# Expert bias as one-pass matmuls over stacked high and low rows; the rows of an expert gated and split when they leave PSUM

## The chip, the cores and the metric

The kernel runs on one core of a Trainium2 chip. The metric is the device time of one execution in microseconds. The engines are named as in the profile: PE is TensorE, DVE is VectorE, ACT is ScalarE, POOL is GpSimd, SP is SyncE, which here mostly issues DMAs.

## The reference, cut to what matters

Two transformer blocks run one after the other on 256 tokens of width 1024. The part that the change touches is the mixture of experts at the end of the first block: every token goes to 4 of 32 experts, each with 1024 x 2048 input weights, a bias of 2048, a clamped SwiGLU, and 1024 x 1024 output weights.

```python
logits = (hf @ w_router + b_router)
top_val, top_idx = lax.top_k(logits, TOP_K)
gates = jax.nn.softmax(top_val, axis=-1)
...
gu = xb @ w1[e] + b1[e]
gate = jnp.minimum(gu[:, :D_FF], SWIGLU_LIMIT)
up = jnp.clip(gu[:, D_FF:], -SWIGLU_LIMIT, SWIGLU_LIMIT)
act = (up + 1.0) * gate * jax.nn.sigmoid(SWIGLU_ALPHA * gate)
return (act @ w2[e] + b2[e]) * g[:, None]
...
out = jnp.zeros((n_tok, d), h.dtype).at[row_tok].add(y.reshape(n_rows, d))
```

All weights are float32: 12 MB for each expert, 32 experts.

## The kernel before, in words

The kernel has three stages. `block_pre` (mixing, memory attention) runs up to about 230 us of the trace; the experts (`route`, `expert_first`, `block_moe`) up to about 1207 us; `post_head` and `block_post` (the second block) after that.

**An expert.** At most 64 tokens (CAP) of an expert are gathered by one-hot matmuls (`gather`, L714, four experts at a time) into columns of 64. `expert_in` first puts the bias into two PSUM banks: four matmuls (L741), each with 32 rows of a selection matrix `bs` (one column of an identity, spread over 64 tokens by a DVE copy, L736) against 32 rows of `b1` (L620 loads it as four blocks of 512 columns, one in each quarter of the partitions). Then 8 weight tiles of 1 MB, 4 matmuls each (L746), are added to the same banks. `gemm1` evicts them (L808 to L812), transposes (L815) and copies (L817) the activations. `gemm2` multiplies them with 4 tiles of output weights, 1 MB each (L829), into one PSUM bank Y with 64 tokens on partitions 0 to 63 for the first 512 output columns and the same tokens on 64 to 127 for the rest. A float32 matmul shows as two records in the trace, a float32r matmul as one; matmuls on 64 columns are issued in pairs that take the two halves of the array.

**Combining.** `rows_out` copies Y to `ysb` on ACT (L834). `combine_weights` transposes the one-hot rows weighted by the gates (`ohw`, L788 on DVE; L800 on PE; L802 on ACT) into `cw`. After every second expert `combine` multiplies `cw` with the `ysb` of both (L845: 8 float32 matmuls on 64 rows, x 2 records) and adds the result to `x` on DVE (L848). The last pair is combined in `post_head` (L1112, L1087).

**Order.** The program order on PE is: input tiles of expert e, output tiles of expert e-1, `combine` after every second one. A list scheduler orders what does not depend, and so slips the bias of the next expert and a gather between other matmuls. SP issues the weight loads in the same order into 12 buffers of 1 MB (3 + 9, `new_w`); a load waits until the matmuls on the tile 12 loads earlier are done. After expert 15 all 12 tiles of expert 16 are loaded ahead and a branch (L880, `If`) skips the path for experts with over 64 tokens; it isn't taken here. `LAST = 2` moves half of the output tiles of expert 30 ahead of expert 31.

## Time and profile before

| | us |
|---|---|
| median of 3 runs | 1553.48 |
| the runs | 1548.6, 1559.29, 1553.48 |
| the profiled execution, and its span | 1548.9, 1547.1 |
| PE busy in the span | 1465.9 (95%) |
| DVE, ACT, POOL busy | 540.0, 384.2, 53.4 |
| moved by DMA | 486.31 MB, mean 314 GB/s |

A share of busy time is an average over the stages. The profile cuts the span into 40 slices of 38.7 us with a digit for each engine, the granted clock of PE and the rate of the DMAs; the experts fill slices 7 to 30. A matmul's end is modelled, so that PE counts as busy for about as long as it has something in flight; whether it waits is seen in the chain of waits.

### The profile page before, as it was taken

How to read it: one execution, taken by the hardware profiler on the slowest of the kernel's cores; microseconds unless marked ns; L12 is line 12 of the kernel's file. 1: busy time of each engine (PE TensorE's matmuls, PEld its weight loads, DVE VectorE, ACT ScalarE, POOL GpSimd, SP SyncE). 2: the span in 40 equal slices, each digit the busy share in tenths (PEclk: the TensorE clock that was granted, in tenths of full speed). 3: DMA queues.
4: the chain of work that ended last, by engine and by line, in shares of the span. 5: the costliest groups of instructions: out<-in, count | busy, mean ns of one | idle time of the engine just before them, and what ended most of it. 6: DMA issues, size and time to landing. Idle time of an engine off the chain costs nothing.

```text
span 1547.1 us, 20381 instructions
## 1 busy us (share of the span) xinstructions
PE 1465.9 (95%) x8440; PEld 798.0 (52%) x8440; DVE 540.0 (35%) x993; ACT 384.2 (25%) x783; POOL 53.4 (3%) x56
## 2 busy tenths in 40 slices
PE   9999999999999999998999999999999975889998
PEld 7899983333333333333333333223323774778998
DVE  5557652111221111121111111211111656985675
ACT  5845441100010010010001000000000553445654
POOL 0010000000000000000000000000000102500000
PEclk9999999999999999999999999999999997999999
DMA  9694347999999999998999999999998453332453
GB/s 336 222 317 164 116 171 285 419 415 417 418 417 413 414 417 416 416 414 343 413 415 419 417 416 417 418 418 415 418 416 334 140 111 98 110 123 94 154 192 108
DMA packets 146498, 486.31 MB, mean 314 GB/s; under 512 B 8606, under 2 KB 77342, under 8 KB 113505
## 3 DMA queue, kind: packets, MB, share of 16 engines
q1 hardware_dynamic: 143968, 479.10, 79.2%
q0 software_dynamic: 1504, 4.12, 1.4%
q10 hardware_dynamic: 928, 1.74, 0.4%
q8 instruction: 68, 1.11, 0.3%
q14 instruction: 30, 0.24, 0.0%
HBM read 481.78 MB, written 3.15 MB: 313 GB/s over the span
## 4 chain that ended last, share of the span: by engine, by line
PE 37%; issue 7%; DVE 5%; DMA 2%; ACT 2%; POOL 0%; POOLq 0%; ACTq 0%; DVEq 0%
PE pP L746 14%; PE pY L829 8%; PE pA L319 4%; PE pP L741 2%; PE pA L845 2%; DMA w<-in_w_in_dram 2%; DVE t L1378 2%; PE pA L714 1%; DVE t L1379 1%; PE pA L815 1%; PE pY L1323 1%; DVE r L1372 1%; DMA w<-in_w_expert_in_dram 0%; PE pP L1691 0%; DVE x L848 0%
## 5 line engine op out<-in xcount | busy, mean ns | idle before, releaser
L746 PE MATMUL pP<-w,xg 128*64 128x512 f32 x2024 | 448.6, 596 | 3.9 <-PEq L880 3.9
L746 PEld LDWEIGHTS pP<-w,xg 128*64 128x64 f32 x2024 | 144.5, 137 | 299.8 <-issue 285.7
L829 PE MATMUL pY<-w,hgu 128*64 128x512 f32 x1024 | 273.1, 606 | 0.7 <-ACT hgu L817 0.7
L209 ACT CAST wh<-w 128x512 fp32r<-128x512 f32 (+1 forms) x256 | 155.1, 615 | 156.2 <-PE pA L319 97.8
L210 DVE TENSOR_TENSOR wl<-w,wh 128x512 fp32r<-128x512 f32 x232 | 157.1, 688 | 76.3 <-ACT wh L209 73.3
L808 DVE TENSOR_SCALAR wh<-pP 128x512 f32<-128x512 f32 x32 | 22.1, 692 | 454.3 <-PE pP L746 454.3
L809 ACT ACTIVATE wh<-wh 128x512 f32<-128x512 f32 x32 | 20.2, 630 | 523.8 <-DVE wh L808 479.8
L829 PEld LDWEIGHTS pY<-w,hgu 128*64 128x64 f32 x1024 | 70.8, 137 | 152.9 <-issue 139.6
L319 PE MATMUL pA<-wh,xh 128*128 128x256 f32 x496 | 142.6, 287 | 4.1 <-DVE bk L1349 4.0
L319 PE MATMUL pA<-wh,xl 128*128 128x256 f32 x496 | 141.7, 286 | 0.0
L319 PE MATMUL pA<-wl,xh 128*128 128x256 f32 x496 | 140.7, 284 | 0.0
L319 PE MATMUL pA<-xh,wh 128*128 128x256 f32 x368 | 108.5, 295 | 4.5 <-ACT wh L209 2.3
L319 PE MATMUL pA<-xh,wl 128*128 128x256 f32 x368 | 106.8, 291 | 2.3 <-DVE wl L210 2.3
L319 PE MATMUL pA<-xl,wh 128*128 128x256 f32 x368 | 105.4, 287 | 0.0
L319 PEld LDWEIGHTS pA<-wh,xh 128*128 128x128 f32 x496 | 95.0, 192 | 5.8 <-issue 3.1
L845 PE MATMUL pA<-ysb,cw 64*128 64x512 f32 x240 | 74.8, 640 | 21.5 <-DVE x L848 11.7
L319 PEld LDWEIGHTS pA<-wl,xh 128*128 128x128 f32 x496 | 94.8, 191 | 0.4 <-issue 0.2
L319 PEld LDWEIGHTS pA<-wh,xl 128*128 128x128 f32 x496 | 94.7, 191 | 0.3 <-issue 0.2
L848 DVE TENSOR_TENSOR x<-pA,x 128x512 f32<-128x512 f32 x60 | 38.8, 686 | 151.1 <-PE pA L845 151.1
L741 PE MATMUL pP<-b,bs 32*64 32x512 f32 x256 | 87.5, 613 | 0.0
L319 PEld LDWEIGHTS pA<-xh,wh 128*128 128x128 f32 x368 | 71.3, 194 | 7.7 <-ACT wh L209 3.5
L319 PEld LDWEIGHTS pA<-xh,wl 128*128 128x128 f32 x368 | 71.3, 194 | 3.6 <-DVE wl L210 3.1
(425 smaller groups left out, 1418.4 us busy)
## 6 DMA issues: line engine op xcount, KB each, us to landing
w<-in_w_expert_in_dram SPq DMA_DIRECT2D x253, 1024.0 KB, 13.5
w<-in_w_expert_out_dram SPq DMA_DIRECT2D x128, 1024.0 KB, 13.1
w<-in_w_in_dram SPq DMA_DIRECT2D x31, 1024.0 KB, 5.4
w<-in_w_mem_kv_dram SPq DMA_DIRECT2D x8, 1024.0 KB, 12.0
w<-in_w_out_dram SPq DMA_DIRECT2D x8, 1024.0 KB, 6.3
w<-in_w_mem_q_dram SPq DMA_DIRECT2D x4, 1024.0 KB, 7.1
w<-in_w_mem_o_dram SPq DMA_DIRECT2D x4, 1024.0 KB, 5.2
w<-in_w_ple_gate_dram SPq DMA_DIRECT2D x4, 1024.0 KB, 4.8
```

Of the source, the lines that this page charges most:

```text
L209: nc.scalar.copy(wh, src)
L210: (nc.gpsimd if lo == "P" else nc.vector).tensor_tensor(wl, src, wh.bitcast(F32), op=ALU.subtract)
L319: nc.tensor.matmul(ps[:, j], lh, rh, start=n == 0, stop=n == tot - 1)
L714: nc.tensor.matmul(ps, xx[tt][:, k * P:(k + 1) * P], og[:, tt], start=n == 0, stop=n == 3)
L741: nc.tensor.matmul(out[i], bs[pr], K.b1[pr], start=True, stop=False, tile_position=(32 * i, 64 * (i % 2)))
L746: nc.tensor.matmul(out[i], xs, raw[:, i * 512:(i + 1) * 512], start=False, stop=k == KT - 1)
L808: nc.vector.tensor_scalar(g, Pb[0], 7.0, None, op0=ALU.min)
L809: nc.scalar.activation(sg, g, AF.Sigmoid, scale=1.702)
L829: nc.tensor.matmul(Y[64 * h:64 * h + 64], act[:, k % 4, k // 4], raw[:, j * 1024 + h * 512:j * 1024 + h * 512 + 512], start=k == 0, stop=k ...
L845: nc.tensor.matmul(pss[h], cws[i][pr, tt], ys[i][pr], start=i == 0, stop=i == 1)
L848: nc.vector.tensor_tensor(xs, pss[h], xs, op=ALU.add)
L1378: TT(pd[:, :, 0:n], BL[:, si:32, si][:, None, :].to_broadcast([P, 16, n]), U[:, si:32].rearrange("p s j -> p j s"), op=ALU.mult)
```

## The change

The bias comes in as two blocks of 1024 columns, each loaded twice (rows 0 to 63 and 64 to 127, 8 loads in place of 4, at the start of the kernel), into buffers that the one-hot rows use later. `bias_split` rounds them to float32r on ACT and leaves on the lower 64 partitions the rest (raw less rounded, on DVE). `bselc` has two columns for each expert, and the bias is two float32r matmuls on all 128 rows, which write 128 columns (both halves) at once.

`combine_weights` transposes the weighted one-hot rows once (64 columns, not 128), makes zeros and ones of them on DVE, copies these to the lower partitions on ACT, and sums the gate of each row on DVE. `rows_out` now scales Y by that gate as it leaves PSUM: for each half of the columns ACT writes the rounded rows (float32r) to 64 partitions and DVE writes the rest to the other 64 (`st`, 5 buffers). `combine` is 8 float32r matmuls on 128 rows. `post_head` does the same for the last pair.

```diff
@@ -52,7 +52,9 @@
     c["before"] = (i[:, None] < i[None, :]).astype(f)
     c["iota_e"] = np.tile(np.arange(NE, dtype=f), (P, 1))
     c["iota_s"] = np.tile(np.arange(CAP, dtype=f), (P, 1))
-    c["bselc"] = np.concatenate([np.eye(NE, dtype=f)] * 4)
+    eye = np.eye(NE, dtype=f)
+    none = np.zeros((NE, NE), f)
+    c["bselc"] = np.block([[eye, none], [none, eye], [eye, none], [none, eye]])
     band = np.zeros((P, 4, 3, P), f)
     for g, win in enumerate((2, 4, 8, 16)):
         full = np.zeros((T, T), f)
@@ -66,7 +68,7 @@
     return {"cpack": pack(c, CPACK), "bpack": pack(c, BPACK).astype(ml_dtypes.bfloat16), "band": band.reshape(P, -1)}
 
 
-WIDTH = {"iota_e": NE, "iota_s": CAP, "bselc": NE, "omask": 64}
+WIDTH = {"iota_e": NE, "iota_s": CAP, "bselc": 2 * NE, "omask": 64}
 
 
 class Pair:
@@ -434,6 +436,7 @@
     mem = K.new_w().rearrange("p (a d) -> p a d", a=2)
     nc.sync.dma_start(mem, A["mem"][0].rearrange("(a p) d -> p a d", p=P))
     moe_load(K, A)
+    bias_in(K, A)
     K.gemm(w_in, 1024, 4, xT, "N", ev_vu, pre=pre_w)
 
     es = []
@@ -576,6 +579,7 @@
     K.gemm(A["w_mem_q"][0], 0, 4, hT, "T", ev_Q, il=True)
 
     ple_load(K, A)
+    bias_split(K)
     ssx2 = K.t([P, 2, 4], F32, "ssx", 2)
     K.hTr = K.t([P, KT, T], F32, "qk", 1)
     lg = K.bank("P", (P, 2, NE))
@@ -611,13 +615,25 @@
 EB = 6
 LAST = 2
 FILL0 = 6
+NST = 5
 
 
 def bias_in(K, A):
     nc = K.nc
-    b1 = K.b1 = K.m([P, 512], F32, "b1", 1)
-    for i in range(4):
-        nc.scalar.dma_start(b1[32 * i:32 * i + 32], A["b_expert_in"][0][:, 512 * i:512 * i + 512])
+    b1 = K.b1 = K.m([P, 2, 512], F32R, "b1", 1)
+    K.b1raw = [K.m([P, 512], F32, "ohr", 2) for _ in range(2)]
+    for b in range(2):
+        for i in range(4):
+            o = 1024 * b + 512 * (i % 2)
+            nc.scalar.dma_start(K.b1raw[b][32 * i:32 * i + 32], A["b_expert_in"][0][:, o:o + 512])
+
+
+def bias_split(K):
+    nc = K.nc
+    lo = slice(64, P)
+    for b, raw in enumerate(K.b1raw):
+        nc.scalar.copy(K.b1[:, b], raw)
+        nc.vector.tensor_tensor(K.b1[lo, b], raw[lo], K.b1[lo, b].bitcast(F32), op=ALU.subtract)
 
 
 def route(K, x, lg, finish):
@@ -732,13 +748,12 @@
 
 def expert_in(K, A, e, spare={}):
     nc = K.nc
-    bs = K.m([P, CAP], F32, "bs", 2)
-    nc.vector.tensor_copy(bs, K.c["bselc"][:, e:e + 1].to_broadcast([P, CAP]))
+    bs = K.m([P, 2, CAP], F32R, "bs", 2)
+    nc.vector.tensor_copy(bs, K.c["bselc"].rearrange("p (j e) -> p j e", j=2)[:, :, e:e + 1].to_broadcast([P, 2, CAP]))
     Pb = [K.bank("P") for _ in range(2)]
     out = [Pb[i // 2][64 * (i % 2):64 * (i % 2) + 64] for i in range(4)]
-    for i in range(4):
-        pr = slice(32 * i, 32 * i + 32)
-        nc.tensor.matmul(out[i], bs[pr], K.b1[pr], start=True, stop=False, tile_position=(32 * i, 64 * (i % 2)))
+    for b in range(2):
+        nc.tensor.matmul(Pb[b], bs.rearrange("p j c -> p (j c)"), K.b1[:, b], start=True, stop=False)
     for k in range(KT):
         raw = spare[k] if k in spare else load_in(K, A, e, k)
         xs = K.XG[e // 4, k][:, e % 4]
@@ -779,13 +794,13 @@
 
     Ys = {}
     OHG = {}
+    cwg = {}
 
     def weigh(g):
-        ow = K.t([P, 2, 4, 2, CAP], F32, "ohw", 2)
-        for tt in range(2):
-            gb = G[:, tt, 4 * g:4 * g + 4, None, None].to_broadcast([P, 4, 2, CAP])
-            og = K.OG[g][:, tt].bitcast(F32)[:, :, None, :].to_broadcast([P, 4, 2, CAP])
-            nc.vector.tensor_tensor(ow[:, tt], og, gb, op=ALU.mult)
+        ow = K.t([P, 2, 4, CAP], F32, "ohw", 2)
+        for tt in range(2):
+            gb = G[:, tt, 4 * g:4 * g + 4, None].to_broadcast([P, 4, CAP])
+            nc.vector.tensor_tensor(ow[:, tt], K.OG[g][:, tt].bitcast(F32), gb, op=ALU.mult)
         OHG[g] = ow
 
     def make_group(g):
@@ -795,12 +810,16 @@
 
     def combine_weights(e):
         g, j = e // 4, e % 4
-        ps = K.bank("A", (P, 2, P))
-        for tt in range(2):
-            nc.tensor.transpose(ps[:, tt], OHG[g][:, tt, j].rearrange("p a b -> p (a b)"), c["ident"])
-        cw = K.t([P, 2, P], F32, "cw", 4)
-        nc.scalar.copy(cw, ps)
-        return cw
+        ps = K.bank("A", (CAP, 2, P))
+        for tt in range(2):
+            nc.tensor.transpose(ps[:, tt], OHG[g][:, tt, j], c["ident"])
+        cw = K.t([P, 2, P], F32R, "cw", 4)
+        gate = K.t([P, 1], F32, "gate", 4)
+        nc.vector.tensor_scalar(cw[0:64], ps, 0.0, None, op0=ALU.is_gt)
+        nc.scalar.copy(cw[64:P], cw[0:64].bitcast(F32))
+        nc.vector.reduce_sum(gate[0:64], ps, axis=AX.XY)
+        nc.scalar.copy(gate[64:P], gate[0:64])
+        return cw, gate
 
     def gemm1(e, spare={}):
         Pb = K.Pb if e == 0 else expert_in(K, A, e, spare)
@@ -829,23 +848,15 @@
                     nc.tensor.matmul(Y[64 * h:64 * h + 64], act[:, k % 4, k // 4], raw[:, j * 1024 + h * 512:j * 1024 + h * 512 + 512],
                                      start=k == 0, stop=k == KT - 1)
 
-    def rows_out(e):
-        y = K.t([P, 512], F32, "ysb", 3)
-        nc.scalar.copy(y, Ys.pop(e))
-        return y
-
     def combine(e):
-        cws = [combine_weights(e - 1), combine_weights(e)]
-        ys = [K.yprev, rows_out(e)]
-        for tt in range(2):
-            pss = [K.bank("A") for _ in range(2)]
-            for i in range(2):
-                for h in range(2):
-                    pr = slice(64 * h, 64 * h + 64)
-                    nc.tensor.matmul(pss[h], cws[i][pr, tt], ys[i][pr], start=i == 0, stop=i == 1)
+        pair = K.yprev, rows_out(K, Ys.pop(e), cwg.pop(e))
+        for tt in range(2):
             for h in range(2):
+                ps = K.bank("A")
+                for i, (cw, st) in enumerate(pair):
+                    nc.tensor.matmul(ps, cw[:, tt], st[h], start=i == 0, stop=i == 1)
                 xs = x[:, tt, h * 512:(h + 1) * 512]
-                nc.vector.tensor_tensor(xs, pss[h], xs, op=ALU.add)
+                nc.vector.tensor_tensor(xs, ps, xs, op=ALU.add)
 
     half = K.nexp // 2 - 1
     prev = None
@@ -863,14 +874,16 @@
         if e % 4 == 3 and e + 1 < K.nexp:
             make_group(e // 4 + 1)
         if prev is not None:
+            cwg[e - 1] = combine_weights(e - 1)
             gemm2(e - 1, prev, ahead2, range(LAST if last else 0, 4))
             ahead2 = {}
             if (e - 1) % 2 == 1:
                 combine(e - 1)
             else:
-                K.yprev = rows_out(e - 1)
+                K.yprev = rows_out(K, Ys.pop(e - 1), cwg.pop(e - 1))
         prev = act
         if e == half:
+            cwg[e] = combine_weights(e)
             gemm2(e, act)
             combine(e)
             prev = None
@@ -880,14 +893,26 @@
             with K.tc.If(cnt > CAP):
                 dense_rest(K, A, x, xh, xl, pos, G, iota_e, g_f)
     last = K.nexp - 1
-    cw = [combine_weights(last - 1), combine_weights(last)]
+    K.cwg = combine_weights(last)
     K.xT = [K.bank("P", (P, 2, T)) for _ in range(4)]
     for k in range(KT):
         for tt in range(2):
             nc.tensor.matmul(K.xT[k // 2][:, k % 2, tt * P:(tt + 1) * P], x[:, tt, k * P:(k + 1) * P], c["ident"],
                              start=k % 2 == 0 and tt == 0, stop=False)
     gemm2(last, prev)
-    K.cw, K.Y = cw, Ys[last]
+    K.Y = Ys[last]
+
+
+def rows_out(K, Y, cwg):
+    cw, gate = cwg
+    st = []
+    for h in range(2):
+        t = K.t([P, 512], F32R, "st", NST)
+        a, b = (slice(64 * i, 64 * i + 64) for i in (h, 1 - h))
+        K.nc.scalar.mul(t[a], Y[a], gate[a])
+        K.nc.vector.scalar_tensor_tensor(t[b], Y[a], gate[a], t[a].bitcast(F32), op0=ALU.mult, op1=ALU.subtract)
+        st.append(t)
+    return cw, st
 
 
 def dense_rest(K, A, x, xh, xl, pos, G, iota_e, g_f):
@@ -1057,7 +1082,6 @@
     c = K.c
     TS, mm = nc.vector.tensor_scalar, nc.tensor.matmul
     w_in = A["w_in_2"][0]
-    y = K.t([P, 512], F32, "ysb", 3)
     s = K.s = K.g([P, 2], F32, "s", 1)
     hs = K.hs = K.g([P, 2], F32, "hs", 1)
     u = K.u = Pair(K)
@@ -1082,9 +1106,8 @@
 
     def spread(tt, h):
         ps = K.bank("Y")
-        pr = slice(64 * h, 64 * h + 64)
-        for i, yy in enumerate((K.yprev, y)):
-            mm(ps, K.cw[i][pr, tt], yy[pr], start=i == 0, stop=i == 1)
+        for i, (cw, st) in enumerate(pair):
+            mm(ps, cw[:, tt], st[h], start=i == 0, stop=i == 1)
         queue.append((ps, x[:, tt, h * 512:(h + 1) * 512]))
 
     def add():
@@ -1103,14 +1126,11 @@
         nc.vector.tensor_tensor(x[:, tt], x[:, tt], gfB, op=ALU.mult)
 
     with K.tc.manual_schedule(engines={nc.scalar.engine, nc.vector.engine}):
-        nc.scalar.copy(y, K.Y)
-        for j in range(4):
-            for h in range(2):
-                k = 4 * h + j
-                pr = slice(64 * h, 64 * h + 64)
-                for i, yy in enumerate((K.yprev, y)):
-                    mm(K.xT[k // 2][:, k % 2], yy[pr, j * P:(j + 1) * P], K.cw[i][pr].rearrange("p a b -> p (a b)"),
-                       start=False, stop=k % 2 == 1 and i == 1)
+        pair = K.yprev, rows_out(K, K.Y, K.cwg)
+        for k in range(KT):
+            for i, (cw, st) in enumerate(pair):
+                mm(K.xT[k // 2][:, k % 2], st[k // 4][:, k % 4 * P:k % 4 * P + P], cw.rearrange("p a b -> p (a b)"),
+                   start=False, stop=k % 2 == 1 and i == 1)
         split(0)
         split(1)
         spread(0, 0)
@@ -1712,7 +1732,6 @@
         xp = K.extra(XW, XH)
         ph = K.phase("pre")
         x, lg, finish = block_pre(K, A)
-        bias_in(K, A)
         with route(K, x, lg, finish):
             expert_first(K, A)
         post_gains(K)
```

**PE, the bias of the next expert, after the input tiles of one expert and around the first output tile of the one before it** (`bs`, `b`: selection and bias; `hgu`: activations; `ohw`: weighted one-hot rows; `pP`, `pY`, `pA`: PSUM banks). Before:

```order
L746 MATMUL pP_3653<-w_3700,xg_3600 64x512 x2
L741 MATMUL pP_3874<-b_397_2522,bs_3872 64x512 x2
L741 MATMUL pP_3875<-b_397_2522,bs_3872 64x512
L829 MATMUL pY_3721<-w_3722,hgu_3565 64x512
L815 MATMUL pA_3714<-cpack_120,wh_3707 128x128 x4
L829 MATMUL pY_3721<-w_3722,hgu_3565 64x512 x3
L800 MATMUL pA_3746<-cpack_120,ohw_3101 128x128 x2
L800 MATMUL pA_3751<-cpack_120,ohw_3101 128x128 x2
L741 MATMUL pP_3875<-b_397_2522,bs_3872 64x512
```

In the changed kernel:

```order
L761 MATMUL pP_3942<-w_3987,xg_3642 64x512 x2
L756 MATMUL pP_4231<-b_77_484,bs_4229 128x512
L756 MATMUL pP_4232<-b_77_484,bs_4229 128x512
L848 MATMUL pY_4017<-w_4018,hgu_3897 64x512 x3
L834 MATMUL pA_4001<-cpack_120,wh_3994 128x128 x4
L815 MATMUL pA_4008<-cpack_120,ohw_3662 64x128 x2
L848 MATMUL pY_4017<-w_4018,hgu_3897 64x512
```

Four matmuls on 64 columns, one of them five places later than the others, become two on 128 columns in one place, and the transposes of `ohw` for this expert alone stand here.

**PE, combining, from the last output tile of an odd expert (`gemm2` ends just ahead) into the first input tile of the next.** Before:

```order
L845 MATMUL pA_3758<-ysb_3648,cw_3749 128x512
L845 MATMUL pA_3759<-ysb_3648,cw_3749 128x512
L829 MATMUL pY_3721<-w_3734,hgu_3565 64x512 x4
L829 MATMUL pY_3721<-w_3740,hgu_3565 64x512 x4
L845 MATMUL pA_3758<-ysb_3756,cw_3754 128x512
L845 MATMUL pA_3759<-ysb_3756,cw_3754 128x512
L845 MATMUL pA_3766<-ysb_3648,cw_3749 128x512
L845 MATMUL pA_3767<-ysb_3648,cw_3749 128x512
L845 MATMUL pA_3766<-ysb_3756,cw_3754 128x512
L845 MATMUL pA_3767<-ysb_3756,cw_3754 128x512
L746 MATMUL pP_3776<-w_3782,xg_3575 64x512 x2
```

In the changed kernel:

```order
L848 MATMUL pY_4017<-w_4036,hgu_3897 64x512 x4
L761 MATMUL pP_4066<-w_4070,xg_3617 64x512
L857 MATMUL pA_4048<-st_4042,cw_4011 128x512
L761 MATMUL pP_4066<-w_4070,xg_3617 64x512
L761 MATMUL pP_4067<-w_4070,xg_3617 64x512
L857 MATMUL pA_4052<-st_4045,cw_4011 128x512
L761 MATMUL pP_4067<-w_4070,xg_3617 64x512
L857 MATMUL pA_4056<-st_3933,cw_3902 128x512
L857 MATMUL pA_4056<-st_4042,cw_4011 128x512
L857 MATMUL pA_4060<-st_3936,cw_3902 128x512
L857 MATMUL pA_4060<-st_4045,cw_4011 128x512
L761 MATMUL pP_4066<-w_4076,xg_3617 64x512 x2
```

The first input tile's matmuls (L746, now L761), which came after all of it, now stand singly between the matmuls that wait for the two halves of `st`.

**ACT, between two evictions of the input matmuls (L809, now L828).** Before:

```order
L809 ACTIVATE wh_5663<-wh_5661 128x512
L817 COPY hgu_5674<-pA_5669 128x512
L802 COPY cw_5704<-pA_5701 128x256
L802 COPY cw_5709<-pA_5706 128x256
L834 COPY ysb_5711<-pY_5676 128x512
L809 ACTIVATE wh_5787<-wh_5785 128x512
```

In the changed kernel:

```order
L828 ACTIVATE wh_5788<-wh_5786 128x512
L836 COPY hgu_5799<-pA_5794 128x512
L819 CAST cw_5804<-cw_5804 64x256
L821 COPY gate_5805<-gate_5805 64x1
L912 ACTIVATE st_5835<-pY_5810,gate_5805 64x512
L912 ACTIVATE st_5838<-pY_5810,gate_5805 64x512
L828 ACTIVATE wh_5913<-wh_5911 128x512
```

For an expert there are now four instructions (L819, L821, L912 twice) for the half of three; DVE has two L913 behind the two L912, and L818 and L820 ahead of L819 and L821.

## Rows read from the trace of the kernel before

**Rows 1.** The page: PE's total, and the DMAs' busy tenths in 40 slices.

```profile
PE 1465.9 (95%) x8440; PEld 798.0 (52%) x8440; DVE 540.0 (35%) x993; ACT 384.2 (25%) x783; POOL 53.4 (3%) x56
...
DMA  9694347999999999998999999999998453332453
```

**Rows 2.** Busy us by stretch; last three columns: granted clock, DMA share, GB/s.

```profile
745.00:1165.00 420.00, 406.60 (x1739) 134.30 (x1737) 66.83 (x114) 35.74 (x69) 0.00 (x0) 1.00 1.02 417
805.00:868.00 63.00, 61.54 (x270) 21.43 (x269) 12.35 (x23) 6.05 (x12) 0.00 (x0) 1.00 1.02 417
868.00:926.00 58.00, 56.48 (x239) 17.87 (x240) 8.65 (x16) 4.25 (x8) 0.00 (x0) 1.00 1.02 417
```

**Rows 3.** Chain of waits, 868 to 926 us: start, us, engine, tile, line.

```profile
868.07 13.88 PE pP L746 x64
881.95 1.86 PE pP L741 x6
...
887.26 1.00 PE pP L741 x2
...
916.06 1.06 PE pA L845 x4
...
920.80 0.59 ACT ysb L834
...
923.35 2.58 PE pA L845 x8
925.92 4.44 PE pP L746 x19
```

**Rows 4.** DMA issues from 860 to 960 us: count, KB, median us to landing.

```profile
w<-in_w_expert_in_dram SPq DMA_DIRECT2D x25, 1024.0 KB, 13.4
```

**Rows 5.** PE's timeline near 279 us: start, us, line, tiles, shape, count.

```profile
278.71 1.09 PE L741 MATMUL pP<-b,bs 32*64 32x512 f32 x8
```

**Rows 6.** Chain of waits, 1150 to 1232 us: float32r matmuls of 256 columns.

```profile
1212.39 1.62 PE pA L1081 x12
```

**Rows 7.** Groups by line: busy, mean ns | idle before.

```profile
L834 ACT COPY ysb<-pY 128x512 f32<-128x512 f32 x31 | 18.2, 586 | 205.0 <-PE pY L829 205.0
L848 DVE TENSOR_TENSOR x<-pA,x 128x512 f32<-128x512 f32 x60 | 38.8, 686 | 151.1 <-PE pA L845 151.1
```

**Rows 8.** SP's timeline at the end of the experts.

```profile
1160.65 15.96 SPq L201 DMA_DIRECT2D w<-in_w_expert_out_dram  x6
```

**Rows 9.** Stretches where the DMAs fall idle; columns as in rows 2.

```profile
256.00:260.00 4.00, 3.69 (x18) 1.33 (x18) 2.77 (x7) 0.59 (x1) 0.00 (x0) 1.00 0.26 77
704.00:710.00 6.00, 6.00 (x26) 1.94 (x24) 2.44 (x6) 1.14 (x3) 0.00 (x0) 1.00 0.44 158
728.00:734.00 6.00, 6.00 (x22) 1.99 (x20) 0.00 (x0) 0.00 (x0) 0.00 (x0) 0.67 0.56 204
...
1184.00:1188.00 4.00, 4.00 (x22) 1.33 (x20) 0.00 (x0) 0.00 (x0) 0.00 (x0) 1.00 1.00 370
1188.00:1192.00 4.00, 4.00 (x25) 2.25 (x22) 2.77 (x4) 0.63 (x1) 0.00 (x0) 1.00 0.42 143
```

**Rows 10.** Chain of waits, 1150 to 1232 us: the last output tiles, the last combining.

```profile
1201.67 5.33 PE pY L829 x24
...
1207.71 2.96 PE pP L1112 x24
```

**Rows 11.** ACT's timeline near 30 us; in brackets idle before, and its releaser.

```profile
30.79 2.30 ACT L209 CAST wh<-w 128x512 fp32r<-128x512 f32 x4 [3.93 <-DMA w<-in_w_in_dram]
```

**Rows 12.** Stretches where PE's granted clock falls; columns as in rows 2.

```profile
415.00:420.00 5.00, 5.00 (x18) 1.73 (x16) 2.10 (x4) 0.59 (x1) 0.00 (x0) 1.00 1.01 418
420.00:425.00 5.00, 5.00 (x14) 1.45 (x14) 1.61 (x3) 0.00 (x0) 0.00 (x0) 0.66 1.02 419
...
1160.00:1165.00 5.00, 3.48 (x17) 0.90 (x13) 0.77 (x2) 0.59 (x1) 0.00 (x0) 1.00 1.01 421
1165.00:1170.00 5.00, 5.00 (x12) 1.99 (x14) 1.90 (x3) 0.00 (x0) 0.00 (x0) 0.66 1.02 423
```

## The prediction

> **What bounds the kernel now.** The page comes first. PE is busy for 95% of the span, and the DMAs' tenths read 9 or 8 in 24 slices in a row, the experts [rows 1]. Two resources look full there, and the question is which of them sets the pace. So the next view is the table of stretches: over 420 us of the experts the DMAs move 417 GB/s at a share of 1.02, in pairs with a gather and without [rows 2]. An expert is 12 loads of 1.0486 MB, a pair 25.17 MB, which is 60.4 us at that rate. The chain of waits gives PE's side: a pair without a gather runs from 868.07 to 925.92, 57.85 us, and nearly every piece of it is PE's own; a pair with a gather lasts 63 us [rows 2, 3]. The mean is 60.4 us as well. PE and the loads are in step to the percent: PE never waits long for a weight, and the loads never run dry.
>
> What decides is the store between them. There are 12 buffers, one expert's worth, so a load is issued one expert (30.2 us) ahead of its use; it lands 13.4 us after its issue [rows 4]. A tile lies in its buffer for 30.2 - 13.4 = 16.8 us before PE comes to it. PE runs 17 us behind the loads, and at the end of the experts this is paid: the last load is issued at 1160.65 + 15.96 = 1176.6 [rows 8], the DMAs are full to 1188 and then fall off, with two 0.5 MB loads of the next stage behind the last expert tile [rows 9], so I put its landing at 1188 (between 1186 and 1189). PE ends the last output tile at 1201.67 + 5.33 = 1207.0 [rows 10], 19 us later.
>
> So PE time taken out of the experts does not shorten them by itself: the loads hold the pace. It gives back this lag at the end, and what the lag cost the loads.
>
> **The change part by part.**
>
> *Bias.* Before, each expert has 8 records, 1.86 us for 6 and 1.00 us for the 2 that the order puts later [rows 3]; a pair costs 5.7 us. Where the 8 stand together they take 1.09 us [rows 5], so a pair costs between 2.2 and 5.7. After, a pair has 4 one-pass matmuls of 512 columns. No row shows that shape; 12 one-pass matmuls of 256 columns take 1.62 us [rows 6], 0.135 each, and twice the columns are at most 0.27: 1.1 us. Saved: 1.1 to 4.6 us for a pair. I take 4.6 in the second half, whose pairs look like rows 3, and 2.5 in the first.
>
> *Combining.* Before: 1.06 us, and 925.92 - 920.80 = 5.1 us after the copy of Y begins [rows 3], 6.2 in all. After: 8 matmuls, 2.2 us, and a longer wait, since the rows go through ACT and DVE. An ACT pass over PSUM takes 0.59, a DVE pass 0.69 [rows 7]; the first half of the rows is ready after 1.28 us, the second after 1.97, and then one DVE add (0.69) must free a bank: 2.2 + 1.97 + 0.69 = 4.8, saved 1.4. If both halves and both adds came one after the other, 2.2 + 2.56 + 1.37 = 6.1 and nothing is saved; if the input matmuls that the order now puts between them cover the wait, 4.0 is saved. I take 1.4, for these input matmuls stand in the same queue behind the waiting ones. On ACT and DVE an expert gets about four more passes of 0.6 us; they are busy 4.25 and 8.65 of 58 us [rows 2], so these hide, except in that wait.
>
> PE then needs 60.4 - 6.0 = 54.4 us for a pair in the second half and 56.5 in the first, against 60.4 for the loads. The lag of 16.8 us is used up in 16.8 / 6.0 = 3 of the 7 pairs behind the branch, and in 4 to 5 of those ahead of it. After that PE waits for every tile: 1.73 us of matmuls (13.88 / 8 [rows 3]) for each 2.51 us of load.
>
> *What it is worth.* (a) The end: the last tile still has its 1.73 us; PE ends at about 1190 in place of 1207, 17 us. (b) The branch: the loads stand idle for 6 x 0.56 = 3.4 us at 704 and 6 x 0.44 = 2.6 us at 728 [rows 9], since PE, 17 us behind and then held at the branch, frees its buffers late. A PE at the loads' heels frees them in time; between 0 and 6.0, I take 5, since the order puts one load more behind the branch. (c) The first loads: 4 x 0.74 = 3.0 us idle at 256 [rows 9], of which the shorter bias ahead of it returns about 1.
>
> *What it costs.* Four more loads of 64 KB at the start, 0.26 MB, are 0.6 us at 417 GB/s. The two casts and two subtractions that split the bias stand among the first weight splits; ACT idles 3.93 us for a weight just after [rows 11], and this hides them: 0 to 1.5, with the loads 0.6. In `post_head` a copy of 0.59 [rows 7] and 2.96 us of matmuls [rows 10] become 1.97 us of passes and 12 one-pass matmuls, 1.6 us, half of which run before the second half of the rows is there: 2.8 to 3.6 against 3.55, so 0. And PE's clock: the granted clock is 0.66 in 1165 to 1170, partly the lower of its two levels, 1.2 in place of 2.4 GHz, right behind a stretch in which PE had waited [rows 12], and a PE that waits for each tile will wait often. The lower level at the very end would cost 1.7 us on the last tile and 1.6 on the last combining; between 0 and 3.3 I take 1.5.
>
> Sum: -17 - 5 - 1 + 0.6 + 1.5 = -20.9 us. The profiled execution took 1548.9 us, its span and 1.8 us around it; that gives 1528. The median of the runs is 4.6 us higher, which would give 1532.6. I forecast 1530.
>
> **The rivals.**
>
> *The clock takes the slack.* The same rows as a mechanism: the clock falls after stretches with waits (1160) and also after full ones with narrow matmuls (415, where PE was busy all the time) [rows 12]. A fall costs 5 x 0.34 = 1.7 us of PE's work. If 2 or 3 come in a pair, most of the 6.0 us are gone, PE stays some 9 us behind, and the branch returns 2: -8 - 2 + 2 = -8, 1541. Against it: a PE that falls behind has no waits left, and the stretches full of input matmuls in rows 2 ran at 1.00. 0.18.
>
> *The clock makes PE the bound: slower.* This decides from 6.0 / 1.7 = 3.5 falls in a pair. With 5, a pair takes 60.4 + 8.5 - 6.0 = 62.9 us, 2.5 more than the loads, and 15 pairs 37 us: 1586. At 1.2 GHz a tile takes 3.5 us against 2.51 for its load, so the pace would really be PE's. Against it is the same: it must go on while PE is never idle. 0.07. The Trainium skill, "TensorE: Matmul & The Clock Gate", section "HAM oscillation", says that a loop whose matmuls on a tile are shorter than the wait for the next tile loses the full clock on every tile. [...]
>
> *The loads go faster once buffers come free early.* The highest rate among the rows is 423 GB/s [rows 12]; 32 experts are 402.7 MB, 965.6 us at 417 and 951.9 at 423: 14 us more gained, 1516. Against it: the share is 1.02 with 13 us of loads in flight already. 0.06. The Trainium skill, "DMA: Bandwidth & Descriptors", section "Where 436 GB/s comes from", puts the ceiling at 435 GB/s, by which an estimate of 925.7 us for the 402.7 MB and a time near 1490 would follow; no stretch here holds it.
>
> *The gain isn't there.* If the first tile's matmuls, broken out of their pairs, and both halves of the rows cost as much as combining saves, and the bias only what it costs in rows 5, a pair gains 1.2 us and the end 1.2 x 7 = 8, less the costs: 1543. 0.12. (If only the one-pass matmuls were two-pass ones, a pair would still gain 2.8 us, enough for the lag.)
>
> **How the numbers follow.** A measurement can tell about 1%, 15.5 us, so faster is below 1538. The forecast has 0.57 (1518 to 1538). Faster: 0.57 + 0.06 + 0.06 of the first rival and the last = 0.69; same: the rest of these, 0.24; slower 0.07. The range goes from 1512, with faster loads, to 1548, the first and the last rival; it leaves out the slower one and some tails.
>
> **What would show it.** DMA share at 1.0 through 704 to 740; PE's idle time before the input matmuls put down to DMAs; loads issued well over 20 us before they land, since buffers free early; last output tile within 3 us of the last landing. Wrong if PE still runs without waiting for weights, if the granted clock in the experts lies clearly below 1.00, or if the rate of the loads moves off 417.

## The result

The changed kernel takes **1533.1 us** (median of 4 runs, 1531.7 to 1533.4); the kernel before took 1556.4 us beside it (1548.6 to 1563.2). The ratio is 0.9866, 95% interval 0.9835 to 0.9896. The forecast was 1530, in a range of 1512 to 1548. The profiled execution of the changed kernel took 1533.0 us with a span of 1531.2; that of before 1548.9 and 1547.1. Between the two profiles lie 15.9 us, between the medians 23.3: the profiled execution of before was among its fastest.

The page of the changed kernel, which answers to [rows 1], with the line of the chain that ended last and the costliest group:

```profile
PE 1415.0 (92%) x8104; PEld 790.1 (52%) x8104; DVE 605.9 (40%) x1123; ACT 416.4 (27%) x849; POOL 52.6 (3%) x56
...
DMA  9695347999999999998999999999999653333453
...
DMA 24%; PE 17%; issue 6%; DVE 4%; ACT 2%; POOL 0%; POOLq 0%; SPq 0%; DVEq 0%; ACTq 0%
...
L761 PE MATMUL pP<-w,xg 128*64 128x512 f32 x2024 | 489.1, 600 | 37.3 <-DMA w<-in_w_expert_in_dram 32.6
```

PE is busy for 51 us less, of which 16 came off the span. The input matmuls (L761) now stand idle for 32.6 us, and that time is put down to the weight loads. The stretches, with the columns of rows 2, answer to [rows 2, 9, 12]:

```profile
745.00:1165.00 420.00, 388.62 (x1620) 131.07 (x1618) 96.98 (x169) 48.80 (x96) 0.00 (x0) 1.00 1.02 416
704.00:710.00 6.00, 5.29 (x18) 1.77 (x17) 3.35 (x5) 1.36 (x2) 0.00 (x0) 1.00 0.61 218
728.00:734.00 6.00, 3.95 (x14) 1.38 (x14) 2.45 (x5) 1.22 (x2) 0.00 (x0) 0.89 1.03 420
...
700.00:704.00 4.00, 4.00 (x20) 1.29 (x17) 0.00 (x0) 0.00 (x0) 0.00 (x0) 1.00 0.42 174
704.00:708.00 4.00, 3.29 (x11) 0.90 (x9) 2.28 (x4) 1.36 (x2) 0.00 (x0) 1.00 0.39 115
...
1204.00:1210.00 6.00, 5.32 (x23) 5.03 (x24) 4.90 (x9) 3.18 (x6) 0.71 (x1) 0.50 0.27 83
```

In the same 420 us PE is busy for 18 us less, the loads move 416 GB/s (before 417), and the granted clock is 1.00. The idle stretch of the transfer engines near the branch is still there, from 700 to 708 (4 x 0.58 + 4 x 0.61 = 4.8 us); the one at 728 is gone.

The chain of waits, which answers to [rows 3], now goes through the loads:

```profile
862.45 20.11 DMA w<-in_w_expert_in_dram
...
882.58 0.02 SPq L203
...
882.63 20.16 DMA w<-in_w_expert_out_dram
...
902.84 19.90 DMA w<-in_w_expert_in_dram
...
922.79 1.96 PE pP L761 x8
```

Every link is one load of 20 us, and the next is issued within 0.1 us of its landing. The time from issue to landing, 13.4 us in [rows 4], is 20.0 now (DMA issues from 860 to 960 us):

```profile
w<-in_w_expert_in_dram SPq DMA_DIRECT2D x29, 1024.0 KB, 20.0
```

Who waits for whom has turned round. SyncE's own queue, from 300 to 1165 us, in the changed kernel (first) and in the kernel before (second): engine, line, what it waited for, us in total, times, longest.

```profile
SPq L203 <- DMA w<-in_w_expert_in_dram: 212.8, 106, 3.5
SPq L200 <- DMA w<-in_w_expert_out_dram: 211.5, 105, 3.2
...
SPq L893 <- SPq L893: 19.5, 1, 19.5
```

```profile
SPq L198 <- PE pP L746: 356.6, 209, 13.3
SPq L201 <- PE pY L829: 232.9, 91, 6.7
```

Before, a load waited for PE to give a buffer back. Now it mostly waits for an earlier load to land.

The end of the experts, PE's timeline of the changed kernel, which answers to [rows 8, 10] (start, us, line, tiles, shape, count; in brackets the idle time before):

```profile
1170.63 1.94 PE L761 MATMUL pP<-w,xg 128*64 128x512 f32 x8 [0.21 <-DMA w<-in_w_expert_in_dram]
...
1184.16 5.37 PE L848 MATMUL pY<-w,hgu 128*64 128x512 f32 x24
1191.09 0.99 PE L1132 MATMUL pP<-cw,st 128*128 128x256 f32 x6 [1.56 <-DVE st L913]
```

PE waits until 1170.6 for the last input tile; six output tiles follow it. The last load of the experts, in the kernel before (first) and in the changed one (second): count, duration in ns, first and last start in us; below it the us from issue to landing (min/median/max).

```profile
L201 SPq DMA_DIRECT2D w<-in_w_expert_out_dram x1: 368/368/368, 1176.2 to 1176.2; - x1
...
DMA to landing us min/median/max: 12.7/12.7/12.7
```

```profile
L203 SPq DMA_DIRECT2D w<-in_w_expert_out_dram x1: 2243/2243/2243, 1167.6 to 1167.6; - x1
...
DMA to landing us min/median/max: 18.4/18.4/18.4
```

It landed at 1188.9 before and lands at 1186.0 now. The last output tile ended at 1207.0 [rows 10] and ends at 1189.5 now. PE's lag behind the last landing has gone from 18.1 us to 3.5.

### The profile page after: what moved, and what is told of

It is laid out like the page before. It is cut to its first block, busy times and chain, and to the rows that moved or that the text cites. A ratio compares the mean times of both kernels' runs of the same rounds, so it can differ in the third digit from the quotient of the medians.

```text
span 1531.2 us, 19893 instructions
## 1 busy us (share of the span) xinstructions
PE 1415.0 (92%) x8104; PEld 790.1 (52%) x8104; DVE 605.9 (40%) x1123; ACT 416.4 (27%) x849; POOL 52.6 (3%) x56
## 4 chain that ended last, share of the span: by engine, by line
DMA 24%; PE 17%; issue 6%; DVE 4%; ACT 2%; POOL 0%; POOLq 0%; SPq 0%; DVEq 0%; ACTq 0%
DMA w<-in_w_expert_in_dram 13%; DMA w<-in_w_expert_out_dram 9%; PE pA L321 5%; PE pP L761 3%; PE pY L848 3%; DMA w<-in_w_in_dram 2%; DVE t L1398 1%; PE pA L730 1%; PE pY L1343 1%; DVE r L1392 1%; DVE t L1399 0%; PE pP L1711 0%; ACT wh L211 0%; PE pA L834 0%; DVE wh L829 0%
## 5 line engine op out<-in xcount | busy, mean ns | idle before, releaser
L761 PE MATMUL pP<-w,xg 128*64 128x512 f32 x2024 | 489.1, 600 | 37.3 <-DMA w<-in_w_expert_in_dram 32.6
L761 PEld LDWEIGHTS pP<-w,xg 128*64 128x64 f32 x2024 | 144.6, 137 | 339.6 <-issue 237.9
L848 PE MATMUL pY<-w,hgu 128*64 128x512 f32 x1024 | 278.9, 606 | 1.4 <-DMA w<-in_w_expert_out_dram 0.7
L827 DVE TENSOR_SCALAR wh<-pP 128x512 f32<-128x512 f32 x32 | 22.1, 692 | 400.4 <-PE pP L761 383.5
L828 ACT ACTIVATE wh<-wh 128x512 f32<-128x512 f32 x32 | 20.2, 631 | 499.2 <-DVE wh L827 499.2
L848 PEld LDWEIGHTS pY<-w,hgu 128*64 128x64 f32 x1024 | 74.2, 137 | 127.4 <-issue 116.8
L913 DVE SCALAR_TENSOR_TENSOR st<-pY,gate,st 64x512 fp32r<-64x512 f32 x64 | 48.0, 750 | 185.6 <-ACT st L912 185.4
L912 ACT ACTIVATE st<-pY,gate 64x512 fp32r<-64x512 f32 x64 | 43.7, 682 | 181.6 <-PE pY L848 155.6
L321 PEld LDWEIGHTS pA<-xl,wh 128*128 128x128 f32 x368 | 72.1, 196 | 0.4 <-issue 0.2
```

The source lines that it names most:

```text
L321: nc.tensor.matmul(ps[:, j], lh, rh, start=n == 0, stop=n == tot - 1)
L761: nc.tensor.matmul(out[i], xs, raw[:, i * 512:(i + 1) * 512], start=False, stop=k == KT - 1)
L827: nc.vector.tensor_scalar(g, Pb[0], 7.0, None, op0=ALU.min)
L828: nc.scalar.activation(sg, g, AF.Sigmoid, scale=1.702)
L848: nc.tensor.matmul(Y[64 * h:64 * h + 64], act[:, k % 4, k // 4], raw[:, j * 1024 + h * 512:j * 1024 + h * 512 + 512], start=k == 0, stop=k ...
L912: K.nc.scalar.mul(t[a], Y[a], gate[a])
```

## The experiments

Each ratio is to the kernel before, run beside it on the same chip. The diffs show the main lines of an edit.

**1. The bias part alone.** The combining is put back to the lines of before, in `combine`, `combine_weights`, `weigh` and `post_head`:

```diff
-        pair = K.yprev, rows_out(K, Ys.pop(e), cwg.pop(e))
+        cws = [combine_weights(e - 1), combine_weights(e)]
+        ys = [K.yprev, rows_out(e)]
```

> Bias matmuls and their loads and split as changed, combining as before. My theory: TensorE's pair of experts was as long as the pair's loads (60.4 us both), so that its lag behind the last load (18.9 us at the end of the last output tile, 1207.0 against a landing near 1188) goes as soon as a pair is over 1 us cheaper; 1.1 to 4.6 us a pair from the bias alone over 16 pairs is 18 to 74 us of slack, so this kernel gets the whole gain: 1531 to 1536 us, as the full change (1533.1). Rival 'additive' (each part gives its own share of 23 us, by its saved TensorE time, bias 4.6 of 6.0): 1538 to 1541. Rival 'the combining does it': 1550 or more.

1535.7 us (1535.0 to 1536.5), ratio 0.9882 (0.9853 to 0.9912). The last output tile ends at 1192.78, 6.4 us behind the last landing (1186.35).

**2. The combining alone.** The bias is put back, with its four row-group matmuls and four loads at the start:

```diff
-    for b in range(2):
-        nc.tensor.matmul(Pb[b], bs.rearrange("p j c -> p (j c)"), K.b1[:, b], start=True, stop=False)
+    for i in range(4):
+        pr = slice(32 * i, 32 * i + 32)
+        nc.tensor.matmul(out[i], bs[pr], K.b1[pr], start=True, stop=False, tile_position=(32 * i, 64 * (i % 2)))
```

> Combining as changed, bias as before (four row-group matmuls, four bias loads at the start). My theory: 1.4 us a pair (bounds 0 to 4.0) over 16 pairs is 22 us of slack against a lag of 15 to 17 us, so most of the gain is here too, and the two parts do not add up: 1533 to 1540 us; and since the bias loads of the start are as before, the pre stage should be 2 to 3 us earlier than in the full change (first load of the up-projection issued near 191.4 and not 194.6). Rival 'additive' (1.4 of 6.0 of the gain): 1549 to 1552 us. Rival 'no saving on TensorE from combining' (its wait for VectorE of 10.1 us over the experts eats it): no change, 1553 to 1557.

1533.4 us (1528.5 to 1538.6), ratio 0.9856 (0.9819 to 0.9893). Its first load of the up-projection is issued at 192.3: 2.3 us earlier than in the full change. The last output tile ends at 1193.72, 3.0 us behind the last landing (1190.77).

These four runs lie 10 us apart, and the profiled one is the slowest of them. From 230 to 244 us its granted clock (third column from the end) reads 0.51, where the changed kernel's reads 0.97, and its first load of the third expert goes out at 264.14, against 256.31 in the changed kernel. That this is what sets the four runs apart is not shown.

```profile
230.00:244.00 14.00, 14.00 (x38) 6.73 (x37) 5.08 (x16) 1.61 (x4) 0.74 (x1) 0.51 0.30 112
```

Each half gives most of the gain by itself: 19.0 and 21.4 us, where both together give 23.3. 'Additive' (1538 to 1541 and 1549 to 1552) falls in both runs.

**3 to 5. Fewer loads.** One tile of an expert's weights in twelve isn't loaded, and PE multiplies the tile before it once more, in the kernel before and in the changed one; then three in twelve in the changed one:

```diff
-            raw = spare[kk] if kk in spare else load_out(K, A, e, kk)
+            raw = raw if kk == 3 else spare[kk] if kk in spare else load_out(K, A, e, kk)
```

```diff
-        raw = spare[k] if k in spare else load_in(K, A, e, k)
+        raw = raw if k in (3, 6) and k not in spare else spare[k] if k in spare else load_in(K, A, e, k)
```

> The kernel before, with the fourth tile of every expert's output weights not loaded: TensorE multiplies the third tile a second time, so all instructions but 32 of 384 expert loads stay, and that twelfth of the weights is left out of the result. A pair's loads fall from 60.4 to 55.4 us. My theory: TensorE set the pace before and the loads waited for it, so next to nothing is gained: 1543 to 1556 us. Rival (loads set the pace in both kernels): 16 pairs x 5.0 = 80 us less, near 1475.

> The changed kernel with the same cut (a twelfth of the expert weights left out of the result). My theory: the loads set the pace after the change, and TensorE needs 54.4 us a pair (forecast) to about 56, so the time falls by 16 x (60.4 - 55.4 to 56.4) = 64 to 80 us, to 1453 to 1470. Rival (TensorE's pair is only just below the loads'): a fall under 20 us, above 1513.

> The changed kernel with a quarter of the expert loads gone (the fourth output tile, and the fourth and seventh input tiles of each expert, each replaced by the tile before it; that quarter of the weights is left out of the result). Loads 45.3 us a pair, so TensorE sets the pace and shows its own pair. At the 54.4 us of the forecast, 16 x 6.0 = 96 us less: about 1437 us; at 56 us, about 1463; TensorE no longer waits for an input tile. Rival: TensorE alone could do a pair much faster (50 us or less): under 1380. Rival, by the clock: without waits TensorE's granted clock falls in the experts and the gain shrinks, above 1480.

One run each: 1551.4, 1481.3 and 1470.4 us. The kernel before gains next to nothing from fewer loads, where 80 us would have come if the loads had set its pace; the changed one falls by 52 with the first cut and by 11 more with the other two. So PE set the pace before, and the loads do after. The fall is smaller than the 64 that I expected. With the first cut the last load lands 67 us earlier (1118.85, against 1186.0), but PE ends 19.2 us behind it (1138.01) and not 3.5: the lag is back. A pair's loads take 55.4 us there, and PE's own pair is not the 54.4 of the forecast, but about as long as these loads. The next two runs share it out.

**6, 7. Each part alone, with a quarter of the loads gone.** The same cuts, in the kernels of 1 and 2.

> The bias part alone, with the quarter of the expert loads gone (that quarter of the weights is left out of the result), so that TensorE shows its own pair: 60.1 us in the kernel before, 55.1 in the full change, so the two parts save 5.0 together, where I forecast 4.6 (bias, bounds 1.1 to 4.6) and 1.4 (combining, bounds 0 to 4.0). By the forecast's sizes the pair here is 55.5 to 56.5 us and the time 1474 to 1492. Rival (the combining saves most, 3 or more): a pair of 58 or more, above 1510.

> The combining alone, with the same quarter of the expert loads gone (left out of the result). By the forecast's sizes TensorE's pair is 58.7 to 59.7 us and the time 1524 to 1543. Rival (the combining saves 3 or more): a pair under 57.5 and a time under 1508. Rival (it saves nothing by itself, since TensorE waits for VectorE's rows): a pair of 60 and a time of 1545 or more.

One run each: 1472.9 and 1493.5 us. PE's own pair is read from the first VectorE pass of an expert (its starts, 13 experts, six pairs, behind the branch). In order: the kernel before with a twelfth of the loads gone, the combining alone, the bias alone, and both, the last three with a quarter gone.

```profile
L808 DVE TENSOR_SCALAR wh<-pP x13: 690/691/692, 789.5 to 1152.3; 128x512 f32<-128x512 f32 x13
```

```profile
L813 DVE TENSOR_SCALAR wh<-pP x13: 690/692/692, 750.5 to 1100.1; 128x512 f32<-128x512 f32 x13
```

```profile
L822 DVE TENSOR_SCALAR wh<-pP x13: 691/692/692, 738.0 to 1079.0; 128x512 f32<-128x512 f32 x13
```

```profile
L827 DVE TENSOR_SCALAR wh<-pP x13: 691/692/692, 741.6 to 1076.2; 128x512 f32<-128x512 f32 x13
```

The last start less the first, over six: 60.5, 58.3, 56.8 and 55.8 us. The loads need 25.17 MB / 416 GB/s = 60.5. PE before was in step with them to a tenth or two (at 417 GB/s they need 60.4). The combining saves 2.2 by itself, the bias 3.6, both 4.7. The time of the combining alone came out 30 us below what I expected: that expectation took 1.4 us for 16 pairs alike. Behind the branch it is 2.2, and ahead of it 4.2: read in the same way over seven pairs, and in the same order, the pairs ahead of the branch take 60.44, 56.20, 55.27 and 54.59 us. So the bias saves 5.2 there, and both together 5.9.

**8. Late bias loads.** The bias rows come late in the first block, by four loads of 128 KB into a weight buffer:

```diff
-    moe_load(K, A)
-    bias_in(K, A)
...
+    bias_in(K, A)
     ple_load(K, A)
     bias_split(K)
...
-    K.b1raw = [K.m([P, 512], F32, "ohr", 2) for _ in range(2)]
+    raw = K.new_w()[:, 0:1024].rearrange("p (b c) -> p b c", b=2)
+    src = A["b_expert_in"][0].rearrange("e (b j c) -> e b j c", b=2, j=2)
+    for i in range(4):
+        nc.sync.dma_start(raw[32 * i:32 * i + 32], src[:, :, i % 2])
```

> The full change, with the bias rows loaded by four 128 KB transfers of SyncE into a weight buffer late in the first block, and split there. If the eight early bias loads are what delayed the first block by 2 to 3 us (first x load issued at 13.85 against 11.27), the first block's later marks come back to those of the kernel before (load of the up-projection issued near 191.4) and the time falls by 2 to 3 us, to about 1530.5. If the delay was in the transfers of that one execution and not in the bias loads: no change, 1532 to 1534. If the late loads and casts cost as much where they are now: 1533 or a little above.

1526.9 us (1525.3 to 1527.7), ratio 0.9822 (0.9793 to 0.9852): 6.3 us better than the change as it was, twice what I expected. Two of SyncE's issues at the start (start, us, line, tiles), in the kernel before, in the changed one, and with late bias loads:

```profile
11.27 3.26 SPq L369 DMA_DIRECT2D x<-in_x_dram  x1
...
191.43 0.38 SPq L1039 DMA_DIRECT2D KTm<-in_w_ple_up_dram  x1
```

```profile
13.85 1.40 SPq L371 DMA_DIRECT2D x<-in_x_dram  x1
...
194.62 0.38 SPq L1064 DMA_DIRECT2D KTm<-in_w_ple_up_dram  x1
```

```profile
11.39 2.92 SPq L371 DMA_DIRECT2D x<-in_x_dram  x1
...
189.90 0.38 SPq L1064 DMA_DIRECT2D KTm<-in_w_ple_up_dram  x1
```

The change had put the first block back by 3.2 us, and the late loads bring it 4.7 forward.

**9. The split late, the loads early.**

```diff
-        nc.scalar.copy(K.b1[:, b], raw)
+        nc.scalar.mul(K.b1[:, b], raw, one)
```

> The full change with its eight bias loads at the start as they were, but the two casts and two subtractions of the split held back (by a factor of one that is only known late) to the end of the first block. Late loads and late split together had brought the first block 4.7 us forward. If 2.7 us of that came from the loads (the first x load issued at 13.85 against 11.39) and 2.0 from the two casts of 0.61 us that ScalarE did in front of weight casts at 20.2 and 21.2, this kernel gets the 2.0: near 1531, with the x load still near 13.8. Rival (all from the loads): 1532.5 to 1534. Rival (all from the casts; the x load's time differs by chance): 1527 to 1528.

1532.4 us (1531.8 to 1532.7), ratio 0.9854 (0.9804 to 0.9904); the x load is issued at 13.62 and the up-projection's at 194.88. The casts cost nothing that these runs show, the loads all of it.

**10. The early loads from GpSimd.** SyncE's waits in the first 56 us of the changed kernel showed bias loads:

```profile
SPq L203 <- DMA ohr<-in_b_expert_in_dram: 5.2, 1, 5.2
...
SPq L127 <- DMA ohr<-in_b_expert_in_dram: 0.7, 1, 0.7
SPq L371 <- DMA ohr<-in_b_expert_in_dram: 0.7, 1, 0.7
```

```diff
-            nc.scalar.dma_start(K.b1raw[b][32 * i:32 * i + 32], A["b_expert_in"][0][:, o:o + 512])
+            nc.gpsimd.dma_start(K.b1raw[b][32 * i:32 * i + 32], A["b_expert_in"][0][:, o:o + 512])
```

> The full change with its eight early bias loads issued by GpSimd in place of ScalarE, at the same place and of the same size; nothing else is moved. Since the late split alone gave nothing, the loss at the start lies with the loads. Theory 'places': the program gives the transfers of SyncE and ScalarE eight semaphores in turn, and each waits until the transfer eight issues before it has landed; in the trace SyncE's first weight loads waited 6.6 us for bias loads. GpSimd's transfers have semaphores of their own, so these waits vanish, the x load is issued near 11.4 and the time is that of the late loads, 1526 to 1529. Rival 'bytes' (0.26 MB more, in small loads, in the fullest stretch of the transfers): the start stays late, x load near 13, 1531 to 1534.

1531.7 us (1528.8 to 1532.3), ratio 0.9863 (0.9814 to 0.9913). None of SyncE's waits falls on a bias load any more, and the start is as late as in the changed kernel: the x load goes out at 14.61, the up-projection's at 194.36. My theory of the places falls. The loads cost by being there: in the traces of all runs the up-projection's load goes out at 189.6 to 189.9 with none of them at the start, at 191.4 to 192.5 with four and at 194.0 to 196.2 with eight.

Their bytes alone don't explain it. Half a megabyte in the first stretch, where the transfers run at 248 GB/s (4 to 8 us in this kernel; 263 with late loads), is 0.52 MB / 0.25 = 2.1 us, an estimate. The x load goes out at 13.2 to 14.6 with eight, but with four, half of these bytes, at 10.9 to 11.6, no later than with none (11.0 to 11.4). What makes the eight cost as much, and how it becomes 4.7 us by the end of the block, stays open. The Trainium skill, "DMA: Bandwidth & Descriptors", section "Rules for kernel authors", wants small transfers joined into one, since below 64 KB one pays mostly overhead; these had 64 KB each and took 5.5 us to land in the changed kernel, but no run here changes their size alone.

**11, 12. The branch.** Its rows in the changed kernel, which belong to SyncE (count, duration in ns, first and last start in us):

```profile
L893 SPq EVENT_SEMAPHORE  x8: 17/17/17, 704.6 to 705.1; - x8
...
L893 SPq COMPARE_BRANCH  x1: 50/50/50, 685.0 to 685.0; - x1
```

SyncE reaches the branch at 685.0 and goes on at 705.1, after eight semaphores: 19.5 us, the time of a landing. It waits until its own loads have landed: the eight semaphores are those that its loads name, and the first of them passes at 704.56, when the load that went out last ahead of the branch (684.60) lands (704.55). Of the 12 tiles that the program loads ahead of it only three go out before it. First I gave GpSimd the first eight loads of the second expert behind the branch, then, on top of run 8's late bias loads, the nine that SyncE issues first:

```diff
-    return K.load_w(A["w_expert_in"][0][e, k * P:(k + 1) * P, :])
+    src = A["w_expert_in"][0][e, k * P:(k + 1) * P, :]
+    if e == K.nexp // 2 + 1 and k < NPOOL:
+        w = K.new_w()
+        K.nc.gpsimd.dma_start(w, src)
+        return w
+    return K.load_w(src)
```

> The full change, with the first eight loads behind the branch in the middle issued from GpSimd in place of SyncE. SyncE stands 19.5 us at the branch, which is the landing time of its last loads (issued by 685, landed by 704.6), and the transfer engines run dry for 4.8 us. If that wait sets the loads back, GpSimd, which passes the branch early, keeps them fed and the time falls by 4 to 5 us, to about 1528.5, with a DMA share of 1.0 from 696 to 712. Rival: GpSimd's loads start no earlier because their buffers come free too late (TensorE holds them): no change, 1533. Rival: loads issued by GpSimd are slower, or it issues them in a worse order: 1535 to 1545.

1532.5 us (1531.0 to 1533.2), ratio 0.9858 (0.9829 to 0.9887): no change, and no test, for SyncE issues nine other loads behind the branch before these, and the transfers stood still as before.

```diff
-            ahead1 = {k: load_in(K, A, e + 1, k) for k in range(KT)}
-            ahead2 = {k: load_out(K, A, e + 1, k) for k in range(4)}
+            ahead1 = {k: load_in(K, A, e + 1, k, nc.gpsimd if k > 2 else None) for k in range(KT)}
+            ahead2 = {k: load_out(K, A, e + 1, k, nc.gpsimd) for k in range(4)}
```

> The changed kernel with the late bias loads, and with the nine loads that SyncE issues first behind the branch (five input and four output tiles of the expert after the branch) given to GpSimd. The eight that were given to GpSimd before were the wrong ones: SyncE itself issued nine others first. If SyncE's 19.5 us at the branch set the loads back by the 4.8 us that the transfer engines ran dry, these nine now go out from 690 on and 3 to 5 us come off the 1526.9 us of the late bias loads: 1522 to 1524. Rival: their buffers come free only as late as the branch, or loads issued by GpSimd take longer to land than they save: 1526 to 1530.

1525.1 us (1523.8 to 1525.6), ratio 0.9796 (0.9743 to 0.9848), the fastest of all. Its stretches (columns of rows 2), which answer to the 700 to 708 above, behind the emptiest of run 8, whose hole lies from 692 to 704 (4 x 0.15 + 4 x 0.76 + 4 x 0.12 = 4.1 us):

```profile
696.00:700.00 4.00, 3.29 (x13) 0.89 (x9) 0.74 (x1) 1.09 (x2) 0.00 (x0) 1.00 0.24 72
```

```profile
696.00:700.00 4.00, 4.00 (x18) 1.14 (x14) 0.00 (x0) 0.66 (x1) 2.97 (x6) 1.00 0.98 399
700.00:704.00 4.00, 3.29 (x10) 0.98 (x10) 2.79 (x4) 0.71 (x2) 1.98 (x3) 1.00 1.01 413
704.00:708.00 4.00, 1.99 (x8) 0.66 (x7) 1.29 (x2) 0.00 (x0) 0.00 (x0) 1.00 1.03 427
```

The hole is filled, so SyncE's wait was its cause. Only 1.8 of its 4.1 us came off, less than I expected, and that is at the edge of what these runs can tell, for the two kernels' runs overlap (1525.3 to 1527.7 with late bias loads alone). The first loads of this profile went out 1.1 us later than there (252.67 against 251.58), and one load of 0.5 MB for the last stage (`b<-in_g_final_dram`), which the other kernels issue at the end of the experts, took part of the hole (issued at 703.58). The rest is not accounted for. SyncE's own next loads then waited for PE to give buffers back (its waits from 680 to 735 us):

```profile
SPq L201 <- PE pP L762: 16.8, 3, 8.7
```

## Why the prediction held, and where it didn't

The sum forecast -20.9 us between the profiles; 15.9 were there. By its own terms:

| term | forecast | measured |
|---|---|---|
| (a) PE's lag at the end | -17 | -14.6 (18.1 to 3.5) |
| (b) the loads at the branch | -5 | -3.7 (load 180 to load 216: 98.7 to 95.0) |
| (c), (d) first loads, extra bias loads | -0.4 | -1.1 (load 36: 304.1 to 303.0) |
| the loads' pace elsewhere | 0 | +1.9 (312 loads: 786.1 to 788.0) |
| (e) `post_head` | 0 | +0.1 (7.6 to 7.7) |
| (f) PE's clock at the end | +1.5 | +1.5 (what is left; the stage behind is 1.4 longer) |

Load n is the n-th of the 384 expert loads to land in the profiled execution; the numbers in brackets are when it lands, or how long it takes from one landing to the other.

**In step, with a lag: right.** PE's own pair before is 60.5 us and the loads' is 60.5 (run 3), so either part alone was enough to use up most of the lag, and the two don't add up (runs 1, 2). Only which of them held the pace was the other way round: the prediction says the loads, and run 3 shows PE. With both of one length this changes nothing in the sum. In the changed kernel PE waits only 1.1 us for input tiles from 300 to 500 us, and 32.4 from 300 to 1165: the lag is gone after some four pairs, as the working had it.

**The pair's saving: 6.0 forecast and 4.7 measured behind the branch, 3.9 and 5.9 ahead of it.** Behind the branch the bias was taken at 4.6, its upper bound, and saves 3.6; the combining was taken at 1.4 and saves 2.2; together 1.1 is lost. Ahead of it the bias was taken at 2.5 and saves 5.2, the combining at 1.4 and saves 4.2. The bias of the changed kernel is dearer than the 1.1 us a pair that the prediction drew from rows 6: PE is busy with it for 30.6 us in 16 pairs, 1.9 each (before, first: 87.5 us, 5.5 each).

```profile
L741 PE MATMUL pP<-b,bs 32*64 32x512 f32 x256 | 87.5, 613 | 0.0
```

```profile
L756 PE MATMUL pP<-b,bs 128*128 128x512 f32 x64 | 30.6, 489 | 9.6 <-DVE wh L829 9.6
```

For the 1.1 us I would look at what PE waits for in the changed kernel, from 300 to 1165 us:

```profile
PE pP L761 <- DMA w<-in_w_expert_in_dram: 32.4, 61, 0.7
PE pA L857 <- DVE st L913: 10.1, 14, 1.0
PE pP L756 <- DVE wh L829: 9.6, 27, 0.4
```

The bias matmul of the next expert, now short, waits 0.36 us for VectorE to leave its bank, once an expert; that this is the loss was not tested. It cost nothing here, since 4.7 is far more than the lag needs.

**(a)** is short by 2.4 us. The last landing before came at 1188.9 and not at 1188, so that there was less lag to give back, and 3.5 us are left, where the working left the last tile's 1.73. Behind the last input tile PE has 18.9 us of work (1170.63 to 1189.53, with the transposes of x), and the loads 15.4. The tile's own matmuls, which I counted, are not what ends last.

**(b) is the step whose mechanism failed**, for the first of its two stretches. It said that a PE at the loads' heels frees its buffers in time and the loads go on through the branch. The buffers were free or nearly so: behind the branch SyncE sends eight loads from 705.2 to 709.2, and its longest wait for PE there is 0.8 us. SyncE was not free. It stands at the branch for its own loads (run 12), and so the first stretch stayed: load 204 landed at 731.3 before and lands at 731.7 now. The wait was in the profile of before too, 15.0 us at its branch (L880), but I looked at what frees a buffer and not at the engine that issues. The second stretch went as forecast: there SyncE had waited 13.3 us for PE, and load 216 landed at 765.7 before and lands at 761.7 now. The DMA share alone would show less, 6.0 to 4.8 us idle, for the transfers of before also ran slower behind that stretch (346 and 344 GB/s from 732 to 740).

**The loads' pace** was taken as unchanged. From load 36 to load 180 and from load 216 to the last it is 1.9 us longer in all, 416 GB/s in place of 417. Why is not known.

**(c) and (d)** have a sum that is 0.7 us off and wrong parts. The four extra loads were put at 0.6 us by their bytes, and the first block ended 3.2 us later (run 8). The experts' start gave back more than the 1 us that I took for a shorter bias: the first load of the third expert is issued at 256.31, against 258.54.

**(e), (f).** From the end of the last output tile to ScalarE's first pass over the finished x, before and after:

```profile
1214.61 1.06 ACT L1100 ACTIVATE hgu<-x 128x1024 bf16<-128x1024 f32 x1 [0.60 <-DVE x L1092]
```

```profile
1197.26 1.06 ACT L1123 ACTIVATE hgu<-x 128x1024 bf16<-128x1024 f32 x1 [0.60 <-DVE x L1115]
```

7.6 us and 7.7. From there to the end it is 332.5 us before and 333.9 now. So what is lost comes later: the granted clock is 0.50 from 1204 to 1210 in the changed kernel, the lower of its two levels, 1.2 in place of 2.4 GHz. The stretch as far behind the last output tile in the kernel before reads 1.00:

```profile
1222.00:1228.00 6.00, 5.13 (x38) 4.59 (x38) 5.40 (x12) 3.87 (x7) 1.08 (x1) 1.00 0.40 114
```

The term has its size, but not the place that I gave it (the last tile and the last combining run at 1.00). That this one stretch is all of it is not shown, for the clock falls again later in both kernels (0.50 from 1275 to 1295 us before, and from 1259 to 1282 now).

**The rivals.** The clock takes nothing in the experts: 1.00 over the 420 us, with PE waiting for tile after tile (only beside the branch it falls: 0.89 from 728 to 734). The Trainium skill, "TensorE: Matmul & The Clock Gate", section "HAM oscillation", has it fall on every tile in a loop where a tile's matmuls are shorter than the wait for the next tile. This loop is not of that kind, so no run here tests the rule: a tile's matmuls take 1.94 us (at 1170.63), and the waits are 0.7 us at the longest. The loads went no faster (416 GB/s). 'The gain isn't there' has a pair gain 1.2 us; the bias alone saves 3.6 and the combining alone 2.2 (runs 6, 7).

**What I said would show it.** PE's idle time at the input matmuls is put down to the loads, as said; the last output tile ends 3.5 us behind the last landing, where I said 3. The DMA share is not 1.0 through 704 to 740, and a load is not issued well over 20 us before it lands, but 20.0.

The forecast itself lies 3 us below the median, and part of that is luck. Of the 20.9 us 5 did not come: (a) 2.4, (b) 1.3 and the pace 1.9, less 0.7 of (c) and (d). But the forecast had added 2 us to its sum of 1528 for the spread of the runs, and these were not due, for the changed kernel's median is that of its profile: its runs lie within 1.7 us, those of the kernel before, where PE sets the pace, within 15.
